# Values turned by VectorE in 32x32 blocks instead of by TensorE, and gate weights fetched a part ahead

## The chip, the cores and the metric

The kernel runs on one core of a Trainium2 chip. A core has TensorE (PE, matmuls, with weight loads shown as PEld), VectorE (DVE), ScalarE (ACT), GpSimd (POOL) and SyncE (SP), which here only issues DMAs; ScalarE issues DMAs too. Each engine works through its own instructions in a fixed order and waits on semaphores for the others. SBUF holds tiles of 128 partitions; TensorE writes PSUM, from which ScalarE and VectorE read. The metric is the device time of one execution in microseconds (us), as the median of several runs; less is better.

## The reference

Two layers work on 1040 tokens of width 1024, 16 learned ones ahead of the 1024 of the input. Each layer has a mixer and a SwiGLU feed-forward part:

```python
proj = h @ w_in
qkv = silu(depthwise_conv_centred(qkv, conv_qkv_w))    # width 3
o_fwd = chunk_gated_delta_rule(qp, kp, vp, ...)
o_bwd = flip(chunk_gated_delta_rule(flip(qp), flip(kp), flip(vp), ...))
y_sc = sc_b * depthwise_conv_centred(sc_c * sc_h, sc_conv_w)
h = h + concatenate([o, y_sc]) @ w_out
gate, up = split(rmsnorm(h) @ w_gate_up, 2)
h = h + (silu(gate) * up) @ w_down
```

`chunk_gated_delta_rule` has 4 heads of 128 channels. It goes over chunks of tokens, solves a triangular system within each and carries a 128x128 state per head from chunk to chunk. What matters here: its values v are needed with the tokens of a chunk on partitions, while the projections leave them with the channels on partitions.

## The kernel before, in words

Activations are kept as rows of 128 channels by 1040 tokens. Every dense product is three matmuls on numbers split in a high and a low part (L156 high weight by high activation, L157 high by low, L158 low by high). A weight tile comes raw over SP's queue into one of two buffers (`raw`, L125), ScalarE rounds it to its high part (`whi`, L126) and VectorE subtracts to get the low part (`wlo`, L127); there are three buffers of each. Results come out of PSUM banks (`pacc`, three of them) through VectorE (L319, L788).

A layer first projects q, k and v and convolves them. The values, one row per head, are made last of these (the loop over `i` that calls `conv` and the silu), and `v_store` (L749 to L766) turns each row into the order of tokens: for the 16 first tokens one transpose on TensorE (L753), a copy by VectorE (L757) and a store (L760); for each half of the other 1024 tokens four transposes of 128x128 (L764) into one PSUM bank, a copy by ScalarE (L765) and a store from ScalarE's queue (L766). They go to the DRAM array `vkd`, nine chunks, each with its values and its keys.

Beside the following projections (z and the short-convolution tiles) run the per-chunk matrices (`chunk_a`, whose L528 adds a triangle to a product), the forward substitution of both directions on VectorE (`substitute`, pairs L560 and L562), and `invert`, which begins with two 32x32-block transposes by VectorE (L571, L572). The substitution of the second direction works in `W` and `Xi`, both buffers of tag `c`. The second smaller tag, `ck2`, has five buffers of 128x512.

Then the scan goes over the chunks in both directions at once. `scan_step` loads the chunk's V, K and A into `rec` (L844, L846, L848), multiplies and adds V (L879, per head) and feeds TensorE (L861). After it come w_out and the sums and differences T1 to T4, B11 to B22 that seven products of a Strassen scheme need (L1044, L1059, L1071, L1092 split weights and activations), and ahead of the seven products the early gate parts: eight weight tiles (`early_part`), each multiplied as soon as its activations stand (L1109, L1112, L1113).

What sets the order: small pieces of work are put in lists (`jobs`, `jobs2`, `jobs3`), one of each is taken after every output chunk of a dense product, and each piece gets a priority. A scheduler then fixes, at build time, the order of every engine and of every DMA queue from these priorities and its own estimate of times. So a change in one piece moves the others' instructions too.

Of the kernel before, what the change touches and what calls it, by code (L numbers as in the profile page):

```python
# [42 lines left out]
def trunk(ctx: ExitStack, tc: tile.TileContext, xT, w_in, w_ba, w_out, w_gu, w_dn,  # L43
# [258 lines left out]
    for l in range(DEPTH):  # L302
# [153 lines left out]

        at0 = [sb.tile([16, 4, 16], F32, tag=f"at0{d}", name=nm("at0")) for d in range(2)]
# [291 lines left out]
        def v_store(i, v, c0):  # L749

            ps = pa()
            if c0 == 0:
                low(lambda: nc.tensor.transpose(ps[0:16, 0:128], v[:, 0:16], ident))  # L753
                vm = t2k("vm")[0:16, 0, :]
                here = tc.cur_priority
                at_prio(evp[0])
                nc.vector.tensor_copy(vm, ps[0:16, 0:128])  # L757
                evp[0] = tc.cur_priority
                at_prio(here)
                dma(vkd[0, 0:16, 0, i * 128:(i + 1) * 128], vm)  # L760
            else:
                vt = v[:, 16 + 128 * (c0 - 1):16 + 128 * (c0 + 3)]
                for c in range(4):
                    low(lambda: nc.tensor.transpose(ps[:, c * 128:(c + 1) * 128], vt[:, 128 * c:128 * c + 128], ident))  # L764
                act(out=vt, in_=ps, func=AF.Copy)  # L765
                adma(vkd[c0:c0 + 4, :, 0, i * 128:(i + 1) * 128].rearrange("c p e -> p c e"), vt.rearrange("p (c e) -> p c e", c=4))  # L766

# [3 lines left out]
        for i in range(4):  # L771
# [7 lines left out]
            jobs.extend([lambda i=i, v=v, c0=c0: v_store(i, v, c0) for c0 in (0, 1, 5)])  # L779
# [25 lines left out]
        for j, q in enumerate((4, 5, 0, 6, 7, 1, 2, 3)):  # L805
# [3 lines left out]
            if j == 3:  # L809
                jobs3.extend(invert(1))  # L810
            if q < 4:
                y3 = sc_tile(q)
            else:
                z_tile(q - 4)
# [24 lines left out]
        def scan_step(d, c, first, final, tied=False):  # L839
# [3 lines left out]
            V, K, A, sz = (rec[:, base + 512 * i:base + 512 * i + 512].rearrange("p (h e) -> p h e", h=4) for i in range(4))  # L843
            dma(V[0:n].rearrange("p h e -> p (h e)"), vkd[c, 0:n, 0, :])  # L844
            if not final:
                dma(K[0:n].rearrange("p h e -> p (h e)"), vkd[c, 0:n, 1, :])  # L846
# [291 lines left out]

        def early_part(f, q):

            A = raw4("raw")
            dma(A, w_gu[l, f, 0, :, 4 * q:4 * q + 4, :])
            w = w_op(A, True)
# [18 lines left out]
        for m in range(KT + 2):  # L1162
# [5 lines left out]
            for f, q in {5: [(0, 0)], 6: [(1, 0)], 7: [(0, 1)]}.get(m, ()):  # L1168
                early_part(f, q)
# [507 lines left out]
```

## Time and profile before

| | |
|---|---|
| runs, median (lowest to highest) | 2463.63 us (2463.17 to 2466.26) |
| profiled execution, time | 2463.0 us |
| its span | 2461.2 us |
| its granted TensorE clock | 0.998 |
| busy: TensorE, weight loads | 2441.9 us (99%), 2255.1 us (92%) |
| busy: VectorE, ScalarE, GpSimd | 1782.3 us (72%), 1056.0 us (43%), 67.0 us (3%) |
| DMA over the span | 135 GB/s |

The span is the profiled execution from its first instruction to its last; the rest of its time lies around it. Rows name the engine, the line of the kernel, the operation and the tiles (out<-in, buffer numbers left out); times in rows are us from the span's start, durations us or, where so said, ns. "[1.23 <-ACT b L765]" is idle time of the engine just before that row and what ended it. Matmuls are pipelined, so a row of a matmul is longer than the distance to the next one.

Layer 0 makes and stores its values between 156 and 212 us, its scan loads begin at 295.39; in layer 1 these are 1392 to 1451 and 1534.61. The early gate parts stand near 560 to 600 and 1790 to 1830.

### The profile page before, as it was taken

The numbers are of one execution on the slowest core, as the hardware profiler recorded it, in microseconds if no ns is written. First come the engines' busy times: TensorE is split into PE (matmuls) and PEld (weight loads), VectorE is DVE, ScalarE is ACT, GpSimd is POOL, SyncE is SP. The second block draws the span as 40 slices with busy tenths as digits, with TensorE's granted clock in tenths as the row PEclk, the third lists the DMA queues.
The fourth block names the chain that finished last, engine by engine and source line by source line (L and its number), as shares of the span: only waits on it lengthen the run. The fifth ranks groups of instructions, "written<-read, shape, count | busy, mean of one in ns | idle before, by whom it ended". The sixth has DMA issues, their size and how long they took to land. (4 is left out here: it accounts for less than half of the span.)

```text
span 2461.2 us, 44853 instructions
## 1 busy us (share of the span) xinstructions
PE 2441.9 (99%) x17530; PEld 2255.1 (92%) x17530; DVE 1782.3 (72%) x3296; ACT 1056.0 (43%) x1964; POOL 67.0 (3%) x157
## 2 busy tenths in 40 slices
PE   9999999999999999999999999999999999999998
PEld 8999999999999999999999988999978888888887
DVE  6888346769877777877657984457697777678774
ACT  6654434535333333444446543335453333234444
POOL 0120000000000000000000200000000000000002
PEclk9999999999999999999999999999999999999999
DMA  4445344534223332674224452445332233237641
GB/s 134 162 156 184 118 134 158 181 102 144 97 95 104 111 104 78 210 239 148 89 87 148 159 178 105 159 142 197 123 124 99 94 116 112 91 107 257 203 131 69
DMA packets 201320, 335.26 MB, mean 136 GB/s; under 512 B 23404, under 2 KB 88356, under 8 KB 201108
## 3 DMA queue, kind: packets, MB, share of 16 engines
q1 hardware_dynamic: 172996, 293.83, 36.0%
q10 hardware_dynamic: 25936, 34.19, 4.3%
q0 software_dynamic: 2176, 4.36, 0.6%
q8 instruction: 138, 2.26, 0.4%
q14 instruction: 74, 0.61, 0.1%
HBM read 250.31 MB, written 81.99 MB: 135 GB/s over the span
## 5 line engine op out<-in xcount | busy, mean ns | idle before, releaser
L156 PE MATMUL pacc<-a,whi 128*128 128x346 f32 (+1 forms) x800 | 260.2, 326 | 0.2 <-ACT a L176 0.2
L158 PE MATMUL pacc<-a,wlo 128*128 128x346 f32 (+1 forms) x800 | 259.0, 325 | 0.1
L156 PE MATMUL pacc<-b,whi 128*128 128x346 f32 (+2 forms) x672 | 232.4, 347 | 0.0
L158 PE MATMUL pacc<-b,wlo 128*128 128x346 f32 (+2 forms) x672 | 231.6, 346 | 0.3 <-DVE wlo L127 0.2
L157 PE MATMUL pacc<-a,whi 128*128 128x346 f32 (+1 forms) x681 | 221.9, 326 | 0.6 <-DVE a L177 0.6
L126 ACT ACTIVATE whi<-raw 128x512 fp32r<-128x512 f32 x166 | 104.6, 632 | 240.5 <-PE pacc L157 194.3
L157 PE MATMUL pacc<-b,whi 128*128 128x346 f32 (+2 forms) x580 | 200.1, 345 | 0.0
L156 PEld LDWEIGHTS pacc<-a,whi 128*128 128x128 f32 x800 | 150.5, 188 | 2.4 <-issue 1.0
L127 DVE TENSOR_TENSOR wlo<-raw,whi 128x512 fp32r<-128x512 f32 x166 | 114.2, 689 | 52.7 <-ACT whi L126 52.0
L158 PEld LDWEIGHTS pacc<-a,wlo 128*128 128x128 f32 x800 | 150.7, 189 | 1.4 <-issue 0.8
L158 PEld LDWEIGHTS pacc<-b,wlo 128*128 128x128 f32 x672 | 126.4, 188 | 10.5 <-issue 1.7
L156 PEld LDWEIGHTS pacc<-b,whi 128*128 128x128 f32 x672 | 126.4, 188 | 9.7 <-issue 0.8
L157 PEld LDWEIGHTS pacc<-a,whi 128*128 128x128 f32 x681 | 128.3, 188 | 4.7 <-issue 2.1
L1091 ACT ACTIVATE whi<-rw 128x512 fp32r<-128x512 f32 x92 | 57.9, 633 | 138.1 <-PE pf L1112 37.3
L157 PEld LDWEIGHTS pacc<-b,whi 128*128 128x128 f32 x580 | 109.2, 188 | 7.9 <-issue 1.0
L1091 ACT ACTIVATE b<-rw 128x512 fp32r<-128x512 f32 x64 | 40.2, 632 | 136.3 <-PE pacc L1112 38.9
L1091 ACT ACTIVATE a<-rw 128x512 fp32r<-128x512 f32 x64 | 40.2, 631 | 103.2 <-PE pacc L1112 62.6
L319 DVE TENSOR_TENSOR b<-pacc,rstd 128x346 f32<-128x346 f32 (+1 forms) x63 | 32.3, 513 | 48.8 <-PE pacc L158 48.7
L1092 DVE TENSOR_TENSOR wlo<-rw,whi 128x512 fp32r<-128x512 f32 x92 | 62.9, 686 | 2.9 <-ACT whi L1091 2.1
L319 DVE TENSOR_TENSOR a<-pacc,rstd 128x346 f32<-128x346 f32 (+2 forms) x59 | 32.7, 554 | 42.4 <-PE pacc L158 42.3
L1113 PE MATMUL pacc<-b,wlo 128*128 128x260 f32 (+1 forms) x172 | 52.7, 306 | 0.0
L1112 PE MATMUL pacc<-b,whi 128*128 128x260 f32 (+1 forms) x172 | 52.7, 306 | 0.0
(965 smaller groups left out, 7846.9 us busy)
## 6 DMA issues: line engine op xcount, KB each, us to landing
raw<-in_w_in SPq DMA_DIRECT2D x110, 256.0 KB
raw<-in_w_gu SPq DMA_DIRECT2D x104, 256.0 KB
rw<-in_w_gu SPq DMA_DIRECT2D x88, 256.0 KB
rw<-in_w_dn SPq DMA_DIRECT2D x94, 192.0 KB
rec<-vkd SPq DMA_DIRECT2D x61, 256.0 KB
raw<-in_w_out SPq DMA_DIRECT2D x48, 256.0 KB
b<-ad SPq DMA_DIRECT2D x45, 260.0 KB
a<-ad SPq DMA_DIRECT2D x45, 256.0 KB
```

The lines of the kernel that those rows point to most:

```text
L126: whi_done[0] = act(out=hi, in_=raw[:, 0:kk, :], func=AF.Copy)
L127: whi_done[1] = tt(out=lo, in0=raw[:, 0:kk, :], in1=hi.bitcast(F32), op=ALU.subtract)
L156: mm(ps[:, :n], wh, xh[:, n0:n1], start=(i == 0), stop=False)
L157: mm(ps[:, :n], wh, xl[:, n0:n1], start=False, stop=False)
L158: last_mm[0] = mm(ps[:, :n], wl, xh[:, n0:n1], start=False, stop=(i == K - 1))
L319: tt(out=t[:, n0:n1], in0=ps, in1=rstd[:, n0:n1], op=ALU.mult)
L1091: act(out=hi, in_=src, func=AF.Copy)
L1092: tt(out=lo, in0=src, in1=hi.bitcast(F32), op=ALU.subtract)
L1112: mm(ps[:, :CW], w[0][:, k, :], tl[:, cs], start=False, stop=False, skip_group_check=True)
L1113: one = mm(ps[:, :CW], w[1][:, k, :], th[:, cs], start=False, stop=stop and k == nk - 1, skip_group_check=True)
```

## The change

The values are no longer turned on TensorE. Each finished row is stored to a DRAM array `vd` as it is (channels by tokens). Once the buffers of the second substitution are free, `v_load` loads it back, two chunks at a time and all four heads side by side (`vm`, 128 x 4 x 256; a small one for the first 16 tokens). `v_turn` transposes 32x32 blocks on VectorE (one STREAM_TRANSPOSE of 128x512 per chunk, `tn`), which leaves channel blocks on partition blocks, and four stores per chunk, one for each 32 partitions, put the blocks in their places in `vkd`. There the four heads now lie next to each other for each channel, so the scan reads the values of one head with a step of 16 bytes. Per layer: 36 transposes on TensorE, four copies on VectorE, eight copies and stores of ScalarE and four stores of SP go; four stores of rows, five loads, nine transposes on VectorE and 36 stores from SP come.

The second part: the weights of an early gate part are loaded and split by `early_weights`, one part ahead of the products that use them. The order of the eight parts stays.

```diff
--- before.py
+++ after.py
@@ -453,6 +453,31 @@
             act(out=kt[0:n].rearrange("p a b -> p (a b)"), in_=ps[0:n], func=AF.Copy)
             adma(vkd[c, 0:n, 1, :], kt[0:n].rearrange("p a b -> p (a b)"))
 
+
+        vd = dram.tile([4, 128, L], F32, name=nm("vd"))
+
+        def v_load(c0, n):
+
+            m = max(n, 32)
+            t = (c4k("vm")[:, 0:4 * m].rearrange("p (h t) -> p h t", h=4) if n > 16 else t2k("vm")[:, :, 0:m])
+            s0 = span(c0)[1]
+            dma(t, vd[:, :, s0:s0 + m].rearrange("h p t -> p h t"))
+            for c in range(c0, c0 + max(n // 128, 1)):
+                vload[c] = t[:, :, 128 * (c - c0):128 * (c - c0) + min(m, 128)]
+
+        def v_turn(c):
+
+            src = vload.pop(c)
+            m = src.shape[2]
+            t = t2k("tn").rearrange("p a b -> p (a b)")[:, 0:4 * m].rearrange("p (j b h) -> p j b h", h=4, b=32)
+            nc.vector.transpose(out=t.rearrange("p j b h -> p h j b"), in_=src.rearrange("p h (j b) -> p h j b", b=32))
+            for i in range(4):
+                if c == 0:
+                    dma(vkd[0, 0:16, 0, 128 * i:128 * i + 128], t[32 * i:32 * i + 16, 0].rearrange("p b h -> p (b h)"))
+                else:
+                    dma(vkd[c].rearrange("(j a) w e -> a j w e", a=32)[:, :, 0, 128 * i:128 * i + 128], t[32 * i:32 * i + 32].rearrange("p j b h -> p j (b h)"))
+
+        vload = {}
 
         at0 = [sb.tile([16, 4, 16], F32, tag=f"at0{d}", name=nm("at0")) for d in range(2)]
         P0 = [sb.tile([16, 4, 16], F32, tag=f"P0{d}", name=nm("P0")) for d in range(2)]
@@ -746,25 +771,6 @@
             mmp[0] = tc.cur_priority
             at_prio(here)
 
-        def v_store(i, v, c0):
-
-            ps = pa()
-            if c0 == 0:
-                low(lambda: nc.tensor.transpose(ps[0:16, 0:128], v[:, 0:16], ident))
-                vm = t2k("vm")[0:16, 0, :]
-                here = tc.cur_priority
-                at_prio(evp[0])
-                nc.vector.tensor_copy(vm, ps[0:16, 0:128])
-                evp[0] = tc.cur_priority
-                at_prio(here)
-                dma(vkd[0, 0:16, 0, i * 128:(i + 1) * 128], vm)
-            else:
-                vt = v[:, 16 + 128 * (c0 - 1):16 + 128 * (c0 + 3)]
-                for c in range(4):
-                    low(lambda: nc.tensor.transpose(ps[:, c * 128:(c + 1) * 128], vt[:, 128 * c:128 * c + 128], ident))
-                act(out=vt, in_=ps, func=AF.Copy)
-                adma(vkd[c0:c0 + 4, :, 0, i * 128:(i + 1) * 128].rearrange("c p e -> p c e"), vt.rearrange("p (c e) -> p c e", c=4))
-
         ca = [0, 1, 8, 2, 7, 3, 6, 4, 5]
         st1 = sub_start(1)
         jobs3.extend([None, None, None, st1[0], st1[1], None, st1[2], st1[3], st1[4]])
@@ -776,7 +782,7 @@
             v = trow() if i % 2 == 0 else row(Y[1] + "f")
             conv(t, v, P_CV + 3 * (8 + i))
             act(out=v, in_=v, func=AF.Silu)
-            jobs.extend([lambda i=i, v=v, c0=c0: v_store(i, v, c0) for c0 in (0, 1, 5)])
+            dma(vd[i], v)
 
         def sc_tile(i):
             t0 = trow()
@@ -808,6 +814,9 @@
                 jobs2.extend([lambda c=c: chunk_a(c) for c in ca])
             if j == 3:
                 jobs3.extend(invert(1))
+                jobs.extend([lambda: v_load(0, 16), lambda: (v_load(7, 256), v_load(1, 256)), lambda: v_turn(0), None,
+                             lambda: (v_turn(8), v_turn(7), v_load(5, 256)), lambda: (v_turn(1), v_turn(2), v_load(3, 256)),
+                             None, None, lambda: (v_turn(6), v_turn(5)), lambda: (v_turn(3), v_turn(4))])
             if q < 4:
                 y3 = sc_tile(q)
             else:
@@ -840,10 +849,12 @@
             n = 16 if c == 0 else 128
             s0 = 0 if c == 0 else 16 + 128 * (c - 1)
             base = d * 2048
-            V, K, A, sz = (rec[:, base + 512 * i:base + 512 * i + 512].rearrange("p (h e) -> p h e", h=4) for i in range(4))
-            dma(V[0:n].rearrange("p h e -> p (h e)"), vkd[c, 0:n, 0, :])
+            V, K, A, sz = (rec[:, base + 512 * i:base + 512 * i + 512] for i in range(4))
+            dma(V[0:n], vkd[c, 0:n, 0, :])
             if not final:
-                dma(K[0:n].rearrange("p h e -> p (h e)"), vkd[c, 0:n, 1, :])
+                dma(K[0:n], vkd[c, 0:n, 1, :])
+            V = V.rearrange("p (e h) -> p h e", h=4)
+            K, A, sz = (t.rearrange("p (h e) -> p h e", h=4) for t in (K, A, sz))
             if c > 0:
                 dma(A.rearrange("p h e -> p (h e)"), aqd[c, d])
                 Zs = [Pv[d][:, (c - 1) * 4 + h, :] for h in range(4)]
@@ -1136,11 +1147,18 @@
         early, bks0 = {}, {}
         turn_e = [None]
 
-        def early_part(f, q):
-
+        EARLY = [(0, 0), (1, 0), (0, 1), (1, 1), (2, 0), (3, 0), (2, 1), (3, 1)]
+        ew = {}
+
+        def early_weights(i):
+            f, q = EARLY[i]
             A = raw4("raw")
             dma(A, w_gu[l, f, 0, :, 4 * q:4 * q + 4, :])
-            w = w_op(A, True)
+            ew[f, q] = w_op(A, True)
+
+        def early_part(f, q):
+
+            w = ew.pop((f, q))
             if q == 0:
                 early[f] = (row(Y[1], F32, 3), row(X[1], F32, 3)) if f < 3 else (row(Y[1] + "f"), c4k())
                 bks0[f] = [pbank() for j in range(NJ)]
@@ -1165,8 +1183,12 @@
             if m == 0:
                 t_split_w(T["B21"], 7, 0)
 
-            for f, q in {5: [(0, 0)], 6: [(1, 0)], 7: [(0, 1)]}.get(m, ()):
-                early_part(f, q)
+            if 5 <= m < 8:
+                early_part(*EARLY[m - 5])
+            if 4 <= m < 8:
+                early_weights(m - 4)
+            if m == 8:
+                early_weights(4)
             k = m - 2
             if k < 0:
                 continue
@@ -1196,8 +1218,10 @@
             t_split(T["T4"], X1, 0, k)
 
 
-        for f, q in ((1, 1), (2, 0), (3, 0), (2, 1), (3, 1)):
-            early_part(f, q)
+        for i in range(3, 8):
+            early_part(*EARLY[i])
+            if 5 <= i + 2 < 8:
+                early_weights(i + 2)
 
         finish_bc(ss, o0, L, rsd[0])
```

The orders move as follows. On VectorE in layer 0, the dense weight splits (L127, `wlo`) near the end of the second substitution (L560/L562 before, L585/L587 after; its two closing transposes are L571/L572 before, L596/L597 after; L319 evicts a dense result, L528/L553 belongs to `chunk_a`). Before:

```order
L127 TENSOR_TENSOR wlo_2745<-raw_2746,whi_2744 128x512
L562 TENSOR_TENSOR x_1565<-x_1565,Tm_1495 128x6x26
L560 TENSOR_TENSOR Tm_1495<-x_1564,x_1565 128x135
L319 TENSOR_TENSOR b_274_2549<-pacc_2698,rstd_81 128x346
L562 TENSOR_TENSOR x_1565<-x_1565,Tm_1495 128x5x27
L127 TENSOR_TENSOR wlo_2873<-raw_2874,whi_2872 128x512
L784 TENSOR_TENSOR b_274_2549<-b_274_2549,rstd_81 128x1040
L528 TENSOR_TENSOR dt_2729<-pb_2724,dt_2729 128x512
L528 TENSOR_TENSOR dt_2733<-pb_2724,dt_2733 128x512
...
L562 TENSOR_TENSOR x_1565<-x_1565,Tm_1495 128x31
L571 STREAM_TRANSPOSE b_326_2964<-x_1565 128x32x32
L572 STREAM_TRANSPOSE x_1564<-x_1565 128x32x32
```

Now:

```order
L587 TENSOR_TENSOR x_1566<-x_1566,Tm_1496 128x31
L596 STREAM_TRANSPOSE b_311_2893<-x_1566 128x32x32
L597 STREAM_TRANSPOSE x_1565<-x_1566 128x32x32
L127 TENSOR_TENSOR wlo_2674<-raw_2675,whi_2673 128x512
L631 COPY b_311_2893<-b_311_2893 32x16x32
L319 TENSOR_TENSOR b_259_2478<-pacc_2627,rstd_81 128x346
L632 COPY b_311_2893<-b_311_2893 32x16x32
L631 COPY b_311_2893<-b_311_2893 32x16x32
L632 COPY b_311_2893<-b_311_2893 32x16x32
L127 TENSOR_TENSOR wlo_2802<-raw_2803,whi_2801 128x512
L553 TENSOR_TENSOR dt_2658<-pb_2653,dt_2658 128x512
L553 TENSOR_TENSOR dt_2662<-pb_2653,dt_2662 128x512
```

The split that is first in the piece before (wlo_2745, now wlo_2674) and all that stood behind it now come after the two transposes.

On SP in layer 0, the raw weight loads of the dense products (L125) and the first value loads (L464, `vm`). L530/L555 store what `chunk_a` made. Before:

```order
L530 DMA aqd_202<-dt_2674 128x512
L125 DMA raw_2880<-in_w_in 128x512
L125 DMA raw_2974<-in_w_in 128x512
L530 DMA aqd_202<-dt_2729 128x512
L530 DMA aqd_202<-dt_2733 128x512
L530 DMA aqd_202<-dt_2781 128x512
L530 DMA aqd_202<-dt_2785 128x512
L348 DMA off_14190<-in_cst 128x256
```

Now:

```order
L348 DMA off_14183<-in_cst 128x256
L464 DMA vm_3037<-vd_215 128x4x256
L125 DMA raw_2809<-in_w_in 128x512
L125 DMA raw_2903<-in_w_in 128x512
L555 DMA aqd_202<-dt_2658 128x512
L464 DMA vm_3039<-vd_215 128x4x256
L555 DMA aqd_202<-dt_2662 128x512
L555 DMA aqd_202<-dt_2710 128x512
L555 DMA aqd_202<-dt_2714 128x512
```

The two raw loads (raw_2880 and raw_2974 before, raw_2809 and raw_2903 now) stand behind the load of a constant tile (L348) and the first load of a pair of chunks.

On VectorE in layer 1, the splits of the early gate weights (L1092 before, L1103 after, with `raw` behind them) among the additions and splits of the Strassen operands (L999, L1059, L1071 before; L1010, L1070, L1082 after). Before:

```order
L1044 TENSOR_TENSOR rstd_19091<-rstd_19091,sq_19724 128x2x256
L177 SCALAR_TENSOR_TENSOR a_1965_19751<-b_1809_18750,par,a_1965_19751 128x512
L999 TENSOR_TENSOR b_1809_18750<-pf_19777,b_1809_18750 128x256
L1059 TENSOR_TENSOR P_1976_19831<-b_1808_18749,P_1976_19831 128x2x512
L1059 TENSOR_TENSOR P_1975_19830<-b_1809_18750,P_1975_19830 128x2x512
L1092 TENSOR_TENSOR wlo_19867<-raw_19864,whi_19866 128x512
L1071 SCALAR_TENSOR_TENSOR b_1809_18750<-b_1809_18750,par,b_1808_18749 128x2x256
L1071 SCALAR_TENSOR_TENSOR b_1808_18749<-b_1809_18750,par,b_1808_18749 128x2x256
L1092 TENSOR_TENSOR wlo_19889<-raw_19886,whi_19888 128x512
```

Now:

```order
L1055 TENSOR_TENSOR rstd_19077<-rstd_19077,sq_19716 128x2x256
L1010 TENSOR_TENSOR b_1807_18736<-pacc_19755,b_1807_18736 128x256
L177 SCALAR_TENSOR_TENSOR a_1966_19743<-b_1807_18736,par,a_1966_19743 128x512
L1103 TENSOR_TENSOR wlo_19815<-raw_19812,whi_19814 128x512
L1010 TENSOR_TENSOR b_1807_18736<-pf_19769,b_1807_18736 128x256
L1070 TENSOR_TENSOR P_1980_19829<-b_1806_18735,P_1980_19829 128x2x512
L1082 SCALAR_TENSOR_TENSOR b_1807_18736<-b_1807_18736,par,b_1806_18735 128x2x256
L1070 TENSOR_TENSOR P_1979_19828<-b_1807_18736,P_1979_19828 128x2x512
L1082 SCALAR_TENSOR_TENSOR b_1806_18735<-b_1807_18736,par,b_1806_18735 128x2x256
L1103 TENSOR_TENSOR wlo_19859<-raw_19856,whi_19858 128x512
```

The split that stood behind the two additions to P_1976 and P_1975 (wlo_19867) is wlo_19815 now and stands ahead of both.

## The prediction

> **What bounds the kernel now.** I read the page first, then the waits of TensorE, then windows of the two stretches that the change touches.
>
> ```profile
> span 2461.2 us, 44853 instructions
> PE 2441.9 (99%) x17530; PEld 2255.1 (92%) x17530; DVE 1782.3 (72%) x3296; ACT 1056.0 (43%) x1964; POOL 67.0 (3%) x157
> PE 43%; DVE 2%; DMA 1%; issue 0%; ACT 0%; DVEq 0%
> ```
>
> TensorE is busy 99% of the span and makes nearly all of the chain that ended last, so its own work is what counts: a microsecond taken from it is a microsecond gained, unless something else is late at that place. The waits of TensorE (in total, times, longest) show how little it waits.
>
> ```profile
> PE pb L1113 <- DVE wlo L1092: 1.7, 2, 1.4
> PE pa L753 <- ACT b L765: 1.2, 1, 1.2
> ...
> PE pf L1113 <- DVE wlo L1092: 0.8, 1, 0.8
> ...
> PE pa L1113 <- DVE wlo L1092: 0.7, 1, 0.7
> PE pf L1109 <- ACT b L1091: 0.6, 1, 0.6
> ...
> PE pa L1109 <- ACT b L1091: 0.5, 1, 0.5
> ```
>
> The 1.2 us at L753 belong to the value transposes, which go. The other five rows, 4.3 us together, are the early gate parts (L1109, L1113), which wait for their split weights.
>
> **The value transposes go (L753, L764).** Four rows of values per layer: each has one transpose of 16 tokens and two groups of four 128x128 ones. The groups, first and last of four rows:
>
> ```profile
> L764 PE MATMUL pa<-ident,b x16: 270/272/273, 161.8 to 200.5; 128*128 128x128 f32 x16
> ...
> L764 PE MATMUL pa<-ident,a3f x16: 270/272/273, 1415.7 to 1448.5; 128*128 128x128 f32 x16
> ```
>
> Matmuls are pipelined, so a group's price is read from starts. One group of layer 1, and the one stall of layer 0:
>
> ```profile
> 1397.84 0.32 PE L157 MATMUL pacc<-b,whi 128*128 128x346 f32 x1
> 1398.01 0.60 PE L764 MATMUL pa<-ident,a 128*128 128x128 f32 x4
> 1398.36 0.40 PE L158 MATMUL pacc<-b,wlo 128*128 128x346 f32 x1
> 1398.60 0.32 PE L156 MATMUL pacc<-b,whi 128*128 128x346 f32 x1
> 1398.76 0.32 PE L157 MATMUL pacc<-b,whi 128*128 128x346 f32 x1
> ...
> 204.61 0.28 PE L753 MATMUL pa<-ident,b3f 128*16 128x128 f32 x1 [1.23 <-ACT b L765]
> ```
>
> From L157 at 1397.84 to the L156 at 1398.60 are 0.76 us with the group; without it the two dense matmuls take 0.32, since one follows the other by 0.16 (1398.60 to 1398.76). A group costs 0.44, a transpose 0.11. 16 groups make 7.0, 8 single ones 0.9, and the stall of 1.23 ends: **9.2 us off TensorE**, 5.2 of it in layer 0, 4.0 in layer 1. This is the firm part, since nothing on TensorE takes its place. The 16 copies of ScalarE (L765) with their 16 stores and the 8 small copies (L757) with theirs go from engines that have room; I count them as nothing.
>
> **The new turns, loads and stores.** The nearest rows to a 32x32 turn are the two transposes that end the substitution in layer 0. I show them with rows of the same stretch that the next step needs:
>
> ```profile
> 233.54 0.68 DVE L127 TENSOR_TENSOR wlo<-raw,whi 128x512 fp32r<-128x512 f32 x1
> ...
> 234.71 0.51 DVE L319 TENSOR_TENSOR b<-pacc,rstd 128x346 f32<-128x346 f32 x1
> ...
> 240.16 1.29 DVE L528 TENSOR_TENSOR dt<-pb,dt 128x512 f32<-128x512 f32 x2
> ...
> 242.32 2.19 DVE L571 STREAM_TRANSPOSE b<-x 128x1024 f32<-128x1024 f32 x1
> 244.41 2.03 DVE L572 STREAM_TRANSPOSE x<-x 128x1024 f32<-128x1024 f32 x1
> ```
>
> 1024 elements take 2.03 to 2.19, so 512 some 1.05 us; eight turns and a small one are 8.7 us of VectorE per layer. They can start only when the loads can, and the big loads take the buffers of the substitution, so after 246.4 in layer 0. The windows (us, then busy time of PE, PEld, DVE, ACT, POOL):
>
> ```profile
> 150.00:234.00 84.00, 82.77 (x927) 79.12 (x926) 75.91 (x174) 41.19 (x57) 6.34 (x12) 1.00 0.45 148
> 246.00:295.00 49.00, 49.00 (x686) 47.46 (x685) 19.95 (x32) 21.30 (x31) 0.00 (x0) 1.00 0.25 88
> 1477.00:1534.00 57.00, 57.00 (x671) 48.81 (x670) 23.90 (x35) 22.07 (x32) 0.00 (x0) 1.00 0.28 100
> 1790.00:1820.00 30.00, 28.59 (x150) 23.10 (x149) 30.00 (x45) 19.80 (x30) 0.00 (x0) 1.00 0.36 119
> ```
>
> Between 246 and 295 VectorE is idle for 29 us, between 1477 and 1534 for 33, and the transfers take a quarter of the DMA engines: 8.7 us of turns fit, at no cost as a sum. Were that cover gone, 17.4 us in both layers would be the price. What remains is order.
>
> **Who comes late: a split behind the substitution.** In the changed order of VectorE the dense split that stood at 233.54 comes after both transposes. TensorE takes it here:
>
> ```profile
> 237.47 0.32 PE L158 MATMUL pacc<-a,wlo 128*128 128x348 f32 x1
> ```
>
> From its end, 234.2, to the end of L572, 246.4, are 12.2 us. Six groups of rows that stood between (the L319 at 234.71 to the L528 pair at 240.16) now come behind, 5.5 us by their durations; 0.4 was idle; so 6.3 us are put ahead of the split. Against that VectorE was idle for 8.1 of the 84 us before (84.00 less 75.91), mostly for results of TensorE that now come sooner, and three copies L757 go, 0.8. The split then ends between 231.6 (all idle time used) and 239.7 (none). TensorE would want it at 237.47, less the 5.2 us, plus 0.9 for nine rows now ahead of it: 233.2. A wait of 0 to 6.5 us. I leave 3 of the 8.1 us idle, since evictions still wait for TensorE: 234.7, a wait of 1.5. The four turns ahead of a later split (L332, L333 stand with them) are 4 us in that idle stretch; layer 1, where VectorE waits more, gets 0.5. **Together +2.0** (0 to 6.5).
>
> **What the loads and stores push.** On SP two raw weight loads of layer 0 now stand behind the first value load, which waits for L572:
>
> ```profile
> 234.25 2.14 SPq L125 DMA_DIRECT2D raw<-in_w_in  x2
> ...
> 250.76 1.16 ACT L126 ACTIVATE whi<-raw 128x512 fp32r<-128x512 f32 x2
> ...
> 295.39 0.33 SPq L844 DMA_DIRECT2D rec<-vkd  x1
> ...
> L861 PE MATMUL pb<-rec,P x24: 267/275/278, 300.5 to 1540.4; 128*128 128x128 f32 x16, 16*16 16x128 f32 x8
> ```
>
> They were issued 16 us before ScalarE used them; scan loads take about 5 us from 295.39 to the first use at 300.5. The transposes end near 234 in the new order, so the loads land by 240: nothing. 36 stores per layer at the 0.33 of such an issue fill 12 us of SP's queue; the last turn ends by 270 and the scan asks at 295, so I count nothing, and some 20 us are the reserve.
>
> **The strided read of the values.** The scan reads V with a step of 16 bytes. Row: L571 reads with a step of 128 bytes, L572 without one, and takes 8% more. All products of the scan that read V, then the second four of one step and the matmul behind them:
>
> ```profile
> L879 DVE SCALAR_TENSOR_TENSOR vv<-pf,negE,rec x64: 329/343/351, 315.5 to 1708.6; 128x128 f32<-128x128 f32 x64
> L879 DVE SCALAR_TENSOR_TENSOR vv<-pb,negE,rec x60: 321/343/352, 314.5 to 1683.3; 128x128 f32<-128x128 f32 x56, 16x128 f32<-16x128 f32 x4
> ...
> 315.49 1.12 DVE L879 SCALAR_TENSOR_TENSOR vv<-pf,negE,rec 128x128 f32<-128x128 f32 x4
> 320.74 0.94 PE L861 MATMUL pf<-vv,P 128*128 128x128 f32 x7
> ```
>
> Four products end at 316.6, 4.1 us ahead. 8% is 0.1 us per four, hidden; a doubled price is 2.2 for both fours, hidden too. I take 0. Here a rule speaks against the change: the Trainium skill, page "SBUF — State Buffer", section "Door 1: The DMA port swizzle", says that SBUF has lines of 16 bytes and that each access to a new line pays. By it every value read is a line of its own; it gives no figure for the penalty, and the 8% of the two rows is all that this trace shows of one. By the rule alone the sum would be the rival of the strided read below.
>
> **Gate weights a part ahead.** In layer 1 the longest of the five waits:
>
> ```profile
> 1803.66 2.36 DVE L1059 TENSOR_TENSOR P<-b,P 128x1024 fp32r<-128x1024 f32 x2
> 1805.93 0.69 DVE L1092 TENSOR_TENSOR wlo<-raw,whi 128x512 fp32r<-128x512 f32 x1
> ...
> 1806.68 0.50 PE L1113 MATMUL pb<-a,wlo 128*128 128x512 f32 x1 [1.41 <-DVE wlo L1092]
> ```
>
> The split now stands ahead of the L1059 pair, so this wait ends. But VectorE is busy 30.00 of 30.00 there: the same work has to be done before the gate products begin, and what the split gains, the additions lose, so TensorE waits a little later instead. The gain lies between 4.3 us and a loss of 5.5 (four splits of 0.69 put ahead in two layers). Nearest to a saturated row is no gain; in layer 0 some should stay: **-1.0**.
>
> **Sum.** 9.2 less 2.0, plus 1.0: 8.2 us gained against the profiled execution's 2463.0 (span 2461.2), 2454.8. The median of the runs is 2463.6, 0.6 above it: 2455.4, rounded 2455.5. 0.2% is 4.9 us, about what a measurement tells from no change.
>
> **The rivals.** (a) VectorE eats the gain: the split waits 6.5 us in layer 0, or the gate stretch loses its 5.5. Time: 2463.6 - 9.2 + 6.5 - 1 = 2460, and 2464 with half of the gate loss (2.7) and no gain there. For it: a VectorE at 75.91 of 84. Against: part of that idle time is waiting for TensorE, which comes sooner. (b) Everything comes: no new waits and the 4.3 us end too, 2463.6 - 13.5 = 2450. Against: VectorE full from 1790 to 1820. (c) Slower: the strided read. Its price decides from 2.8 times on, where two fours use up the 4.1 us of room; at four times two fours lose 6.7 - 4.1 = 2.6 us per step, and the 124 products, 31 fours, are 15.5 such steps: 40 us, less 8.2, 2495. Slower by over 0.2% it is from 3.2 times on (0.85 us a step, 13 in all). For it: every element in another line. Against: L571 and L572. (d) The transposes' removal changes nothing because it was hidden: against it stands TensorE's 99%.
>
> **How the numbers follow.** The forecast (2452 to 2458.7) gets 0.50, (b) 0.10, (a) 0.27, (c) 0.12, (d) 0.01 and ends within 0.2%. Faster is the forecast and (b), 0.60; same (a) and (d), 0.28; slower (c), 0.12. The range goes from (b), 2450, to past the end of (a), 2465; (c) beyond it is left out. The likeliest case's own range is 2452 to 2459.
>
> **What would show it.** Right: 72 matmuls fewer on TensorE and its busy time about 8 us less; turns of about 1.05 us between 246 and 290 in layer 0; at most one new wait of 1 to 3 us near 230 for a split (wlo, L127); the scan's products near 343 ns as before. Wrong: turns above 1.5 us; waits of TensorE for splits or raw loads between 230 and 265 of over 5 us; first scan loads later than 295 less the gain; L879's successor well above 343 ns; gate waits that only moved.

## The result: slower by a quarter of a per cent

In 15 runs of each kernel, the changed kernel takes 2470.74 us (median, 2468.94 to 2475.21), the kernel before 2465.66 us (2461.03 to 2466.88). The ratio is 1.0025 with a 95% interval of 1.0018 to 1.0032. The prediction was 2455.5 us in a range of 2450 to 2465, with a chance of 0.12 for slower by over 0.2%. In the profiled executions the span grew from 2461.2 to 2467.6 us, by 6.4, where the prediction had 8.2 less.

The page of the changed kernel (span, busy time of the engines):

```profile
span 2467.6 us, 44819 instructions
PE 2442.4 (99%) x17458; PEld 2252.5 (91%) x17458; DVE 1805.5 (73%) x3306; ACT 1046.6 (42%) x1948; POOL 67.4 (3%) x157
```

The 72 matmuls are gone (17530 to 17458), but TensorE is busy 0.5 us longer than before, not 8 us less. So something made other matmuls slower. The waits of TensorE (in total, times, longest) hold a second part of the loss:

```profile
PE pacc L158 <- DVE wlo L127: 4.3, 4, 2.4
PE pa L1120 <- ACT b L1102: 1.3, 1, 1.3
...
PE pacc L1120 <- DVE a L1010: 1.1, 1, 1.1
PE pf L649 <- ACT P L656: 1.1, 1, 1.1
...
PE pf L647 <- ACT b L630: 0.7, 1, 0.7
...
PE pf L156 <- ACT whi L126: 0.6, 1, 0.6
...
PE pf L647 <- ACT b L654: 0.5, 1, 0.5
```

The waits at the early gate parts and at the first of the seven products fell from 4.3 to 2.4 us, all of it now at L1120; 0.6 comes new at a product of w_out beside them (L156). The dense splits (L158 waiting for wlo) and the steps of the inversion (L647, L649) are new.

**The slow matmuls.** The timeline of TensorE at the start of the scan in layer 0 (start, duration, instruction). Here L872 is the line that was L861, and the last row is the first group in the kernel before:

```profile
301.86 1.98 PE L872 MATMUL pb<-rec,P 128*128 128x128 f32 x8
303.48 0.52 PE L158 MATMUL pacc<-a,wlo 128*128 128x346 f32 x1
...
304.08 1.97 PE L872 MATMUL pf<-rec,P 16*16 16x128 f32 x8
305.98 0.44 PE L157 MATMUL pacc<-a,whi 128*128 128x346 f32 x1
...
309.38 0.46 PE L157 MATMUL pacc<-a3f,whi 128*128 128x346 f32 x1
309.67 0.33 PE L158 MATMUL pacc<-a,wlo 128*128 128x346 f32 x1
309.83 0.32 PE L156 MATMUL pacc<-a,whi 128*128 128x346 f32 x1
```

```profile
300.50 1.05 PE L861 MATMUL pb<-rec,P 128*128 128x128 f32 x8
```

Two things are to be seen. A group of eight matmuls that reads the values straight from `rec` takes 1.98 us; the same group took 1.05 before. And the dense matmuls behind the groups start 0.29 us apart instead of 0.16, from 305.98 to 309.67, and wait for nothing. The windows (busy time of PE, PEld, DVE, ACT and POOL with their instructions, then the granted clock, the share of the DMA engines and GB/s) say why; the last row is the stretch behind the groups in the kernel before:

```profile
301.80:305.90 4.10, 4.10 (x20) 2.68 (x18) 0.00 (x0) 1.63 (x5) 0.00 (x0) 1.00 0.76 270
305.90:309.70 3.80, 3.80 (x15) 3.73 (x15) 0.00 (x0) 1.11 (x4) 0.00 (x0) 0.55 0.74 214
1544.70:1548.90 4.20, 4.20 (x20) 2.70 (x18) 1.41 (x2) 1.63 (x5) 0.00 (x0) 0.98 0.99 302
1548.90:1552.20 3.30, 3.30 (x12) 3.28 (x12) 0.00 (x0) 1.11 (x4) 0.00 (x0) 0.51 0.27 93
```

```profile
304.00:308.00 4.00, 4.00 (x31) 4.00 (x31) 0.52 (x1) 0.17 (x1) 0.00 (x0) 1.00 0.67 199
```

Right behind the two slow groups the granted clock falls. The means of 0.55 and 0.51 depend on where the windows are cut; the clock records of the trace hold 0.50 for 3.41 us in either layer, from 306.26 and from 1548.71. In the kernel before the clock stays at 1.00 there in both layers.

Two instructions read the values: TensorE's first step and VectorE's products. Grouped by line (duration of one: least, median, most):

```profile
L872 PE MATMUL pb<-rec,P x24: 383/405/409, 301.9 to 1546.4; 128*128 128x128 f32 x16, 16*16 16x128 f32 x8
L872 PE MATMUL pf<-rec,P x16: 380/400/403, 304.1 to 1548.6; 16*16 16x128 f32 x16
L890 DVE SCALAR_TENSOR_TENSOR vv<-pf,negE,rec x64: 419/436/468, 320.6 to 1718.3; 128x128 f32<-128x128 f32 x64
```

VectorE's products went from 343 to 436 ns, and TensorE waits for them once, 0.3 us. TensorE's own 40 matmuls (24 and 16) went from 275 to about 403 ns, and their starts from 0.11 to 0.23 us apart (1.05 less 0.28 over seven, 1.98 less 0.40 over seven).

**Where the 6.4 us are.** For the two profiles I summed, by line and shape, the distances from one start on TensorE to the next:

| part | predicted | in the trace after, less before |
|---|---|---|
| value transposes and their stall | -9.2 | -7.9 (matmuls 6.7, stall 1.2) |
| waits of layer 0, 205 to 255 us | +1.5 | +4.5 (0.7, 0.5, 1.1, 1.4, 0.5, 0.3) |
| wait of layer 1 at 1516 us | +0.5 | +2.4 |
| strided reads of TensorE, 5 groups of 0.93 | 0 | +4.6 |
| lower clock behind them | 0 | +3.1 (layer 0: 13 starts in 3.69 us, less 13 times 0.16; layer 1: 11 in 3.29) |
| gate parts | -1.0 | -2.0 (layer 0 0.0, layer 1 -2.0) |
| the rest (waits of 0.2 to 0.5 us elsewhere) | 0 | +1.7, what is left |

**The waits.** In layer 0 TensorE (first three rows) comes to steps of the inversion whose inputs ScalarE has not evicted, and then (fourth row) to a dense split:

```profile
211.49 1.14 PE L647 MATMUL pf<-b,P 64*64 64x64 f32 x16 [0.69 <-ACT b L630]
219.47 0.27 PE L647 MATMUL pf<-b,P 64*64 64x64 f32 x1 [0.53 <-ACT b L654]
227.71 1.14 PE L649 MATMUL pf<-P,b 64*64 64x64 f32 x16 [1.12 <-ACT P L656]
238.78 0.43 PE L158 MATMUL pacc<-a,wlo 128*128 128x348 f32 x1 [1.40 <-DVE wlo L127]
...
208.54 1.07 ACT L759 ACTIVATE b<-b 128x1040 f32<-128x1040 f32 x1 [1.66 <-DVE x L587]
...
216.88 1.90 ACTq L552 DMA_DIRECT2D dt<-dtd  x2
218.83 1.08 ACT L654 ACTIVATE b<-pf 64x512 f32<-64x512 f32 x2 [4.96 <-DVE Tm L585]
```

In ScalarE's order a Silu (L759) and loads for the attention products (L552, which wait for VectorE by the rows, 4.96 us) now stand ahead of the evictions. The fourth wait, 1.40, is the split behind the substitution. In layer 1 VectorE, SyncE's queue and TensorE:

```profile
1513.54 1.99 DVE L473 STREAM_TRANSPOSE tn<-vm 128x512 f32<-128x512 f32 x2 [5.97 <-DMA vkd<-tn]
1515.37 0.68 DVE L127 TENSOR_TENSOR wlo<-raw,whi 128x512 fp32r<-128x512 f32 x1
...
1503.97 5.04 SPq L478 DMA_DIRECT2D vkd<-tn  x6
...
1509.60 5.35 SPq L478 DMA_DIRECT2D vkd<-tn  x9
...
1516.10 0.50 PE L158 MATMUL pacc<-b,wlo 128*128 128x512 f32 x1 [2.43 <-DVE wlo L127]
```

Two turns wait 6 us for their buffers, which are free only when the stores of earlier turns are done; a split whose other half (`whi`) was done by 1509.5 stands behind them.

### The profile page after: what moved, and what is told of

Same layout as the page of the kernel before. It is cut to its first block, busy times and chain, and to the rows that moved or that the text cites. A ratio compares the mean times of both kernels' runs of the same rounds, so it can differ in the third digit from the quotient of the medians.

```text
span 2467.6 us, 44819 instructions
## 1 busy us (share of the span) xinstructions
PE 2442.4 (99%) x17458; PEld 2252.5 (91%) x17458; DVE 1805.5 (73%) x3306; ACT 1046.6 (42%) x1948; POOL 67.4 (3%) x157
## 5 line engine op out<-in xcount | busy, mean ns | idle before, releaser
L156 PE MATMUL pacc<-a,whi 128*128 128x346 f32 (+1 forms) x800 | 261.3, 327 | 1.1 <-ACT a L176 0.5
L158 PE MATMUL pacc<-a,wlo 128*128 128x346 f32 (+1 forms) x800 | 259.8, 326 | 1.7 <-DVE wlo L127 1.7
L158 PE MATMUL pacc<-b,wlo 128*128 128x346 f32 (+2 forms) x672 | 232.1, 346 | 2.7 <-DVE wlo L127 2.6
L156 PE MATMUL pacc<-b,whi 128*128 128x346 f32 (+2 forms) x672 | 232.7, 347 | 0.0
L156 PEld LDWEIGHTS pacc<-a,whi 128*128 128x128 f32 x800 | 151.2, 189 | 4.4 <-issue 1.3
L158 PEld LDWEIGHTS pacc<-a,wlo 128*128 128x128 f32 x800 | 151.2, 189 | 3.5 <-DVE wlo L127 2.6
L127 DVE TENSOR_TENSOR wlo<-raw,whi 128x512 fp32r<-128x512 f32 x166 | 114.0, 687 | 43.0 <-ACT whi L126 42.1
L158 PEld LDWEIGHTS pacc<-b,wlo 128*128 128x128 f32 x672 | 127.0, 189 | 13.1 <-DVE wlo L127 3.6
L156 PEld LDWEIGHTS pacc<-b,whi 128*128 128x128 f32 x672 | 127.0, 189 | 9.9 <-issue 0.8
L1103 DVE TENSOR_TENSOR wlo<-rw,whi 128x512 fp32r<-128x512 f32 x92 | 62.8, 685 | 3.0 <-ACT whi L1102 2.2
L319 DVE TENSOR_TENSOR b<-pacc,rstd 128x346 f32<-128x346 f32 (+1 forms) x63 | 32.3, 512 | 39.5 <-PE pacc L158 39.3
L319 DVE TENSOR_TENSOR a<-pacc,rstd 128x346 f32<-128x346 f32 (+2 forms) x59 | 32.6, 552 | 31.8 <-PE pacc L158 31.7
L1120 PE MATMUL pacc<-b,whi 128*128 128x260 f32 (+1 forms) x172 | 52.7, 306 | 1.1 <-DVE a L1010 1.1
```

The costliest lines, as they stand in the source:

```text
L127: whi_done[1] = tt(out=lo, in0=raw[:, 0:kk, :], in1=hi.bitcast(F32), op=ALU.subtract)
L156: mm(ps[:, :n], wh, xh[:, n0:n1], start=(i == 0), stop=False)
L158: last_mm[0] = mm(ps[:, :n], wl, xh[:, n0:n1], start=False, stop=(i == K - 1))
L319: tt(out=t[:, n0:n1], in0=ps, in1=rstd[:, n0:n1], op=ALU.mult)
L1103: tt(out=lo, in0=src, in1=hi.bitcast(F32), op=ALU.subtract)
L1120: one = mm(ps[:, :CW], w[0][:, k, :], th[:, cs], start=first and k == 0, stop=False, skip_group_check=True)
```

## The experiments

**Theory S: strided reads of TensorE.** The slow groups and the lower clock come from TensorE reading its moving operand with a step of 16 bytes. It was put alone on the kernel before, with a control that has the same instructions in the same order.

```diff
             if first:
-                r = V
+                r = vn                                                 # b_copy
+                r = vv[:, 0:512].rearrange("p (e h) -> p h e", h=4)    # b_strided
+                act(out=r[0:n], in_=V[0:n], func=AF.Copy)
```

The extra product of the first chunk reads a copy in the same way.

> The kernel before, whose values lie contiguous, with one thing added: the values that TensorE reads directly (first scan step of either direction, and the extra product of the first chunk) are first copied by ScalarE to a contiguous tile, and TensorE reads the copy. It is the control for the run with the strided copy. Theory S (strided reads of TensorE cost the time): no strided read here, so as the kernel before, within 1 us. Rival Q (the slow first step comes from the order of the queues and the later loads, not from the stride): also as before. In both a matmul of the first step starts 0.12 us after the one ahead of it, and the granted clock stays at 1.00 there.

> As the control with the contiguous copy, same instructions in the same order, but the copy lies in the changed kernel's layout (step of 16 bytes from one element to the next of a head). Theory S: 40 matmuls that start 0.238 instead of 0.122 us apart, 4.6 us, and the granted clock falls to about 0.55 for some 3.7 us right behind the two strided groups of either layer, another 3.2 us: 7.8 us slower than the control, ratio about 1.0032. Rival S1 (the stride costs, but the dip of the clock has another cause, such as the stores or the order ahead of the scan): 4.6 us slower, no dip. Rival Q: as the control.

Measured: the control 2466.41 us, ratio 1.0008 (0.9999 to 1.0017); strided 2472.66 us, 1.0034 (1.0021 to 1.0048); 6.3 us apart. The timeline of either, first the control:

```profile
302.02 1.05 PE L861 MATMUL pb<-vv,P 128*128 128x128 f32 x8
303.47 1.04 PE L861 MATMUL pf<-vv,P 16*16 16x128 f32 x8
```

```profile
301.95 1.98 PE L861 MATMUL pb<-vv,P 128*128 128x128 f32 x8
304.33 1.97 PE L861 MATMUL pf<-vv,P 16*16 16x128 f32 x8
```

The windows, first the control and then the strided one, the second stretch of each layer being the one behind the groups:

```profile
302.00:305.90 3.90, 3.90 (x30) 3.38 (x29) 0.00 (x0) 3.21 (x10) 0.00 (x0) 1.00 0.85 307
305.90:309.60 3.70, 3.70 (x30) 3.70 (x29) 1.21 (x2) 0.63 (x1) 0.00 (x0) 1.00 0.56 152
```

```profile
306.20:309.90 3.70, 3.70 (x14) 3.67 (x14) 0.52 (x1) 1.11 (x4) 0.00 (x0) 0.54 0.49 140
1551.80:1555.20 3.40, 3.40 (x14) 3.40 (x14) 0.52 (x1) 1.11 (x4) 0.00 (x0) 0.59 0.37 135
```

Groups and dips are those of the changed kernel (0.50 for 3.41 us again), without turns, loads and new stores. S holds, with 6.3 us where it gave 7.8; S1 and Q fall.

**The other way round:** the changed kernel with the contiguous copies (as `b_copy`; VectorE goes on reading with the step).

> The changed kernel, with the same contiguous copies ahead of TensorE's first scan step; VectorE goes on reading the values with the step of 16 bytes, and turns, loads, stores and early weights stay as they are. Theory S: 7.8 us faster than the changed kernel, so about 2463, some 1.5 us under the kernel before; the clock stays at 1.00 at the scan's start in both layers. Rival S1: 4.6 us faster, and the dips of the clock stay. Rival V (VectorE's strided read is what costs): as the changed kernel.

Measured: 2465.9 us, 1.0008 (0.9998 to 1.0018), 4.8 us under the changed kernel's median (4.2 by the two ratios); the profiled span fell by 7.3 to 2460.3, and the clock is 1.00 at both places. So this one read made the kernel slower than before; without it the change is worth nothing that can be measured. V falls.

**What of the stride costs, and what makes the clock dip.** Two variants of `b_strided`: two heads interleaved instead of four (a step of 8 bytes), and only the backward direction's copy strided.

```diff
-                r = vv[:, 0:512].rearrange("p (e h) -> p h e", h=4)
+                r = vv[:, 0:512].rearrange("p (g e k) -> p g k e", g=2, k=2)                    # b_stride8
+                r = vv[:, 0:512].rearrange("p (e h) -> p h e", h=4) if d else vn                # b_half
```

> As the control with the contiguous copy, but the copy lies with a step of 8 bytes from one element to the next. If the price goes by lines of 16 bytes, a line is read for every two elements: a matmul of the first step starts between 0.12 and 0.24 us after the one ahead of it, by half of the lines 0.12 to 0.15; if any step beyond one element costs the full price, 0.238. At 0.12 the granted clock should stay at 1.00 at the scan's start, at 0.238 it should dip in both layers.

> The kernel before with the copies ahead of the first scan step, of which only those of the backward direction (the eight matmuls of the last chunk) lie with the step of 16 bytes; the others lie contiguous. The eight start 0.238 us apart, 0.9 us in either layer. Theory W (the clock dips because TensorE does little in a stretch of some 4 us, with both strided groups in it): with one group no dip in either layer, the clock stays at 1.00. Rival T (any strided group triggers it): the dip of about 3.7 us follows the eight matmuls in both layers.

`b_stride8` took 2469.81 us and `b_half` 2469.47 in the one run that each had, too few to tell their times; they are read by their profiles. The groups with a step of 8 bytes, in layer 1:

```profile
1547.93 1.07 PE L861 MATMUL pb<-vv,P 128*128 128x128 f32 x8
1548.93 1.08 PE L861 MATMUL pf<-vv,P 16*16 16x128 f32 x8
```

8 bytes cost nothing, 16 double the time, and at 8 bytes no dip follows in either layer. With one strided group (`b_half`), the group and then the windows ahead of it and behind it in layer 0, behind it in layer 1, and one at another place:

```profile
303.37 1.98 PE L861 MATMUL pb<-vv,P 128*128 128x128 f32 x8
305.75 1.04 PE L861 MATMUL pf<-vv,P 16*16 16x128 f32 x8
```

```profile
303.30:306.80 3.50, 3.50 (x22) 2.82 (x20) 0.00 (x0) 1.54 (x6) 0.00 (x0) 1.00 0.95 351
306.80:310.30 3.50, 3.50 (x22) 3.50 (x23) 0.52 (x1) 1.27 (x6) 0.00 (x0) 1.00 0.61 155
...
1549.20:1552.70 3.50, 3.50 (x24) 3.50 (x23) 0.52 (x1) 1.09 (x5) 0.00 (x0) 1.00 0.26 98
205.20:208.70 3.50, 3.42 (x13) 3.42 (x14) 1.74 (x7) 1.79 (x4) 0.00 (x0) 0.52 0.34 90
```

The slow group stays and no dip follows it, so rival T as it stands falls. Theory W fits, but that both groups are needed is not shown. The clock records of all 14 profiles say more: every dip ahead of the end of the kernel is 0.50 for 3.41 us (one lasts twice that), and every change of the clock lies a whole number of 3.413 us behind the first one of its profile. These stretches begin at another place in each profile (4.0 to 7.1 us of the span). In the stretch ahead of the four dips of the changed kernel and of `b_strided`, 10 to 13 slow matmuls start; the stretches with 3 to 6 of them have no dip behind them. In `b_half` the eight lie on both sides of a boundary, five and three, in both layers. Eight in one stretch did not occur, and the forward group was not run alone.

The last row of the windows shows that the clock can dip elsewhere: here behind the stall at L753, the 1.2 us that the value transposes have before the change. It did so in this profile and in that of `b_early`, and not in those of the kernel before, `b_copy`, `b_strided` and `b_stride8`. Near 56 us, long ahead of the values (156 us), five of the 14 profiles have a dip and nine have none; `b_stride8` has the double one there, which can be a part of its 2469.81. A single profile is therefore good to one to three dips of 1.6 us, and the sizes above are better taken from the runs: 6.3 us and 4.8 us, where the trace alone gives 7.7.

**The second part alone:** the early gate weights on the kernel before (the last pieces of the change's diff, in short):

```diff
-            w = w_op(A, True)
+            w = ew.pop((f, q))
...
+            if 4 <= m < 8:
+                early_weights(m - 4)
```

> The kernel before with the second part of the change alone: the early gate weights a part ahead. The prediction gave it -1.0 us (bounds -4.3 and +5.5). The trace of the changed kernel reads as -2.0 us in layer 1 (the wait for the split of 1.4 and two smaller ones gone, 1.3 of it back for the next evicted sum) and 0 in layer 0 (two waits of 1.5 gone, two new ones of 1.7): -2 us, ratio 0.9992. If the early splits push VectorE's additions back as the rival said, 2 to 5 us slower.

Measured: 2465.12 us, 1.0005 (0.9996 to 1.0014). And the same lines turned back in the changed kernel with contiguous copies:

> The changed kernel with the contiguous copies and without its second part: each early gate part loads and splits its weights itself, as before. The prediction gave the second part -1.0 us; the kernel before with this part alone came out 0.0005 above the kernel before (interval 0.9996 to 1.0014). Reading of the traces: in the run with the contiguous copies TensorE waits 1.6 us in layer 0 and 1.3 in layer 1 at the early gate parts, in the kernel before 1.5 and 2.8; so without the second part 0 to 2 us slower than with it. If it is faster by over 1 us, the second part loses time, as the rival of the gate stretch said.

Measured: 2464.19 us, 0.9999 (0.9990 to 1.0008), where `a_contig` stood at 1.0008. No gain by the second part in either pair. In layer 1 the kernel before waits 1.7 us for splits of early weights and 1.1 (L1109 for L1091) at the first of the seven products, whose weights ScalarE rounds from `rw`; `a_contig` waits 1.3 at the latter place alone (L1122 for L1104). In layer 0 it is 1.6 us (1.0 for a PSUM bank that VectorE empties, 0.6 at w_out) against 1.5. So the traces have 4.3 us before and 2.9 in `a_contig`, but 2.7 in `c_noearly`, which has no early weights: within the changed kernel the waits only changed their cause.

**The removal alone:** what the transposes were worth.

```diff
...
-                for c in range(4):
-                    low(lambda: nc.tensor.transpose(ps[:, c * 128:(c + 1) * 128], vt[:, 128 * c:128 * c + 128], ident))
-                act(out=vt, in_=ps, func=AF.Copy)
                 adma(vkd[c0:c0 + 4, :, 0, i * 128:(i + 1) * 128].rearrange("c p e -> p c e"), vt.rearrange("p (c e) -> p c e", c=4))
```

> The kernel before with the value transposes and ScalarE's and VectorE's copies of them left out: the rows are stored as they lie, with stores of the same size, so the scan computes on blocks of the values that are not transposed. It measures what the removal of this work from TensorE is worth by itself. The prediction said 9.2 us (ratio 0.9963). Theory E (the inversion of layer 0 was hidden behind the transposes): the matmuls and the one stall are worth 7.9 us, but without them TensorE comes to the inversion's steps before ScalarE has evicted their inputs, and loses there again some 2.3 to 4.5 us as in the changed kernel: 3.4 to 5.6 us gained. Rival O (the waits of layer 0 come from the turns, loads and stores): the full 7.9, and no waits of TensorE between 205 and 250 us.

Measured: 2455.22 us, 0.9962 (0.9950 to 0.9975), 8.7 us under the kernel before. The line of the engines on its page:

```profile
PE 2434.5 (99%) x17458; PEld 2248.4 (92%) x17458; DVE 1779.8 (73%) x3288; ACT 1046.6 (43%) x1948; POOL 66.3 (3%) x157
```

TensorE's busy time falls by 7.4, and it has no wait between 200 and 275 us. Theory E falls: the inversion is not late because its cover is gone. But the first three waits of the changed kernel (211 to 228 us) lie ahead of the first turn (255 us) and the first value load (238.2 us), so these cannot hold TensorE there either. What is left, by the rows and not by a run of its own, is the order of ScalarE: here the Silu stands behind the evictions L604 and L605, in the changed kernel ahead of them. No run moved the Silu or the loads L552 alone, and why the changed program gets the other order was not tried.

**The waits one by one.** On `a_contig`, half of the stores on GpSimd's queue; then also one chunk more between the last steps of the first inversion (the edit does so in both layers; the waits were in layer 0); then GpSimd's queue in layer 1 only:

```diff
+            two = (dma, qdma)                          # x_pool, x_gap
+            two = (dma, qdma if l else dma)            # x_gap1
...
-                    dma(vkd[c].rearrange("(j a) w e -> a j w e", a=32)[:, :, 0, 128 * i:128 * i + 128], t[32 * i:32 * i + 32].rearrange("p j b h -> p j (b h)"))
+                    two[i // 2](vkd[c].rearrange("(j a) w e -> a j w e", a=32)[:, :, 0, 128 * i:128 * i + 128], t[32 * i:32 * i + 32].rearrange("p j b h -> p j (b h)"))
...
-[lambda a=a, b=b: fourth_fifth(a, b) for a, b in (((0, 1), ()), ((2, 3), (0, 1)), ((), (2, 3)))]
+[f for a, b in (((0, 1), ()), ((2, 3), (0, 1)), ((), (2, 3))) for f in [None] * (1 - d) + [lambda a=a, b=b: fourth_fifth(a, b)]]   # x_gap, x_gap1
```

> The changed kernel with the contiguous copies, and half of the stores of the turned values issued by GpSimd's queue instead of SyncE's. Theory B (in layer 1 two turns wait 6 us for their buffers, which the stores free late since SyncE issues them one by one, and a split waits behind the two turns): the wait of TensorE for that split, 2.6 us near 1513, goes, and the time falls by 2 to 2.6 us against the run with contiguous copies alone. Rival L (the turns wait for their loads): no change, the wait stays. Rival G: GpSimd's issues are so slow that the scan's first loads come late and the start of the scan waits.

Measured: 2466.57 us, 1.0010 (1.0001 to 1.0019), no gain. The mechanism was right and the sum was not: the wait at 1513 us is gone, but the order of VectorE moved in layer 0 too, where a split now stands behind two turns. The waits of this kernel from 200 to 275 us:

```profile
PE pacc L158 <- DVE wlo L127: 3.9, 3, 1.6
PE pf L649 <- ACT P L656: 1.1, 1, 1.1
PE pf L647 <- ACT b L630: 1.0, 1, 1.0
PE pf L647 <- ACT b L654: 0.5, 1, 0.5
PE pacc L156 <- ACT whi L126: 0.4, 1, 0.4
```

> As the run with half of the stores on GpSimd's queue, and in layer 0 the last three steps of the first inversion each wait one dense chunk longer before they are issued. Theory E: the three waits of TensorE at these steps, together 2.0 to 2.4 us between 211 and 229, go, since the evictions have a whole chunk of time; the end comes some 2 us earlier, unless the later inversion makes the second one or the attention products late. Rival O: the waits only move.

Measured: 2461.01 us, 0.9991 (0.9982 to 1.0000), 5.6 us under `x_pool`; ten of the eleven runs lie between 2458 and 2466, one took 3767 us for a reason that is not known. The same window has one wait left:

```profile
PE pacc L158 <- DVE wlo L127: 1.9, 1, 1.9
```

The three waits of the inversion are gone, and with them those of the splits at 240 and 254 us: 6.9 us of waits became 1.9. So the waits of layer 0 are real time, they come from where the steps stand, and they can be moved away. The wait that is left costs more than itself here: the clock drops to 0.50 for 3.41 us right behind it, from 263.9.

> As the run with the longer gaps between the inversion's steps, but GpSimd's queue issues half of the stores in layer 1 only; in layer 0 all stores are SyncE's again. If the split that TensorE waits for near 263 to 268 in layer 0 (1.6 to 1.9 us) is late because the stores on GpSimd's queue let the turns move ahead of it, that wait goes and the time is 1.5 to 2 us under the run with the gaps, about 2459, and 0.2% under the kernel before. If the split is late because of the turns and their loads in either order, the wait stays and the time is as in the run with the gaps.

Measured: 2461.51 us, 0.9988 (0.9979 to 0.9997). The split's wait stays (1.4 us at 262), as the second reading had it. What holds the two turns ahead of it is not the same: a load in `x_gap` (1.50 us, vm<-vd), the stores of earlier turns in `x_gap1` (2.77 us, vkd<-tn), as in layer 1 of the changed kernel.

**A version that beats both:** `x_gap1` without the second part of the change (the lines of `b_early` turned back).

> As the run with the gaps and with GpSimd's queue in layer 1 only, but without the second part of the change (each early gate part loads its own weights, as before). The pair with the contiguous copies stood at 1.0008 with the second part and 0.9999 without it, with intervals that overlap. If the second part really costs some 2 us, this kernel comes 2 us under the run with it, about 2459.5 and 0.2% under the kernel before. If it is worth nothing, it stays at 2461 to 2462; if it gains the 1 to 2 us that the waits in layer 1 showed, it comes at 2463.

Measured: 2458.79 us, 0.9982 (0.9973 to 0.9991), 4.8 us under the kernel before. It still has a wait of 3.0 us for the split at 263 us, and a dip of the clock there (0.50 for 3.41 us). Against `x_gap1` it is the third pair in which the kernel without early weights is lower (0.0005, 0.0009, 0.0006); no pair shows it alone, and a cost of some 1.6 us is likelier than the gain of 1.0.

## Why the prediction was wrong

- **"9.2 us off TensorE"** held: 8.7 us in the run that takes away this alone, 7.9 in the trace of the changed kernel.
- **"The strided read of the values ... I take 0"** is the step that failed and turned the sign. It costed the read at VectorE's products alone, and there it was right that the price is hidden: 343 ns became 436 (27%, not 8%), and TensorE waited 0.3 us in all. But the list of readers was not complete: the first step of the scan has no products, and TensorE reads `rec` itself. The row of these matmuls (L861, pb<-rec,P) was even quoted, for the time of the loads. That read costs 4.6 us in 40 matmuls and some 3 us by the lower clock; the runs give 4.8 to 6.3 together. So rival (c), slower by the strided read, had the right place and the wrong reader: it asked for 2.8 times the price on VectorE, where 1.27 times was paid.
- The rule of the Trainium skill that the prediction weighed and set aside (page "SBUF — State Buffer", section "Door 1: The DMA port swizzle") was the better guide as far as it asks for at least two accesses to a line of 16 bytes for full bandwidth. The runs agree for TensorE: two to a line (8 bytes) 1.07 us, one to a line (16 bytes) 1.98 us per eight. The 8% of the two transposes said nothing about TensorE's read.
- **"The split stands behind the substitution, 1.5 us in layer 0"**: 1.40 us, at 238.78. The place was said to be 233.2: the split ended at 238.7 and not at 234.7, and TensorE came to it at 237.4, so both were some 4 us later than worked out, and that the difference fits is in part luck. In layer 1 the 0.5 was nothing of this kind.
- **"8.7 us of turns fit, at no cost as a sum" and "36 stores ... I count nothing"** failed in layer 1. The turns took what was said (1.08 us). The 36 stores took 18.8 us of SP's queue in layer 0 and 18.7 in layer 1 where the prediction had 12 (0.44 each in the median, not 0.33), and the scan's loads were still issued in time. But the reserve was counted to the wrong end: not the scan, the next turn waits for the stores, 6.0 us, and a split behind it on VectorE makes TensorE wait 2.4.
- **Missing:** the 2.3 us at the inversion's steps (0.69, 0.53, 1.12). The prediction followed VectorE's order, not ScalarE's. In sum the new waits, 4.5 us in layer 0 and 2.4 in layer 1, are about as long as rival (a) had them (6.5), but that is luck: (a) had one split late in layer 0, and splits make only 4.1 of the 6.9.
- **"Gate weights a part ahead, -1.0"**: three pairs of runs show no gain. That the waits only move, as the step itself argued, is what the rows show. And not all of the 4.3 us belonged to the early parts: the two rows of L1109 (1.1 us) are the first of the seven products, which take weights rounded from `rw`, so the gain could be 3.2 at most.

## What to carry to other kernels

When a change alters a layout, list every instruction that reads the tile, on every engine and in the first and last step of a loop, before you price the stride; one row of the page that names the tile as an input is enough to find them. Work taken from the bound engine is gained only if nothing that it waits for is reordered by it: look at the order of the engines that feed it, eviction by eviction, and not only at their idle time. And a store counts up to whoever waits for its buffer, not up to whoever reads its data.

## What the runs showed of the hardware

- A matmul of 128 columns in fp32 whose moving operand has a step of 16 bytes takes twice as long (1.98 us for eight against 1.05); with a step of 8 bytes it takes the same (1.07). VectorE's product of 128 elements pays 27% for the 16 bytes.
- Slow reads can cost the clock. Where 10 to 13 of these slow matmuls start within 3.41 us, the granted clock falls to 0.50 for the next 3.41 us (four of four, in two kernels), though TensorE shows as busy all the time; behind 3 to 6 of them it stays at 1.00. The Trainium skill (page "TensorE: Matmul & The Clock Gate", section "Part 1: The HAM clock gate") has a gate that halves the clock after an idle window of some 3.4 us, a window that runs freely. The length, the depth and the grid of 3.413 us agree; that the clock falls where TensorE is shown as busy is what the trace adds.
- The dip behind the stall of 1.2 us at L753 came in two of six profiles that have the stall, and the one near 56 us in five of 14. In those five the stretches of 3.413 us begin at 4.35 to 5.28 us of the span, in the other nine at 3.96 or at 5.21 and later. So the same part of a program loses some 1.6 us or not, it seems by where these stretches fall.
